# Keys of dilated attention stored by their residue modulo 16, in a hybrid decoder layer

## The chip, the cores and the metric

One NeuronCore of a Trainium2 chip runs the whole layer. The metric is device time in microseconds for one execution. Before the change the median of three runs is 2245.28 us (2243.73 to 2248.41).

## The reference

The layer takes x of 2048 tokens by 1024. After a norm, one projection feeds 8 attention heads and 8 heads of a gated linear recurrence (HGRN), each 64 wide; both outputs are normed, projected and added to x, and a two-level mixture of experts and a last norm follow. The change concerns the attention, which evaluates three dilated windows and mixes them by their log-sum-exp:

```python
DILATED_CONFIGS = ((128, 1), (512, 4), (2048, 16))
def dilated_branch(q, k, v, slopes, window, dilation):
    # query t attends keys t - j*dilation, j = 0..window/dilation
    ...
    scores = jnp.einsum('bgnqhd,bgnkhd->bgnhqk', qb, kk) / math.sqrt(Dh)
    bias = -slopes[:, None, None] * (sub_dist * dilation)[None]
    scores = jnp.where(valid, scores + bias, -jnp.inf)
    lse = jax.nn.logsumexp(scores, axis=-1)
    o = jnp.einsum('bgnhqk,bgnkhd->bgnqhd', jnp.exp(scores - lse[..., None]), vv)
```

For a branch of dilation d the tokens fall into d residue classes, and a block is 128 queries of one class against the 128 keys of its own block and the 128 before.

## The kernel before, in words

Heads are worked on in four pairs. For each pair the kernel projects v, q and k from a normed and transposed x (`v_tile`, `qk_chunk`), runs 48 attention blocks (`attention_steps`: 16 of branch 1, then 16 of branch 3, whose step is 16, then 16 of branch 2, whose step is 4; the names in the code are `br` 1, 3 and 2, with `DIL` their steps), and beside them projects and runs the pair's HGRN heads (`hgrn_steps`, `quad_steps`). Precision is held by splitting operands into a high and a low half of 16 bits.

`qk_chunk` projects 512 tokens into a PSUM tile ("proj", two buffers) and evacuates it for each of the two heads: ScalarE writes the high half (L358), VectorE the low half (L359). Tokens lie side by side in their own order, in `k` as in `qs`; for k, GpSimd's queue then copies both halves to the other 64 partitions (L361). `v_tile` leaves v in an SBUF tile V whose rows are tokens; branch 1 reads that tile itself. It is also spilled to DRAM (`vd`, L396), from where `load_v` reads it back in the row order of branch 3 and of branch 2 (L408, on SyncE's queue).

One block is `scores` and, three blocks later, `values`. `scores` issues four matmuls (L436): for each of the two heads the 128 queries are loaded as weights and the block's 128 or 256 keys stream through, once for the high and once for the low half of k. `block_cols` gives both operands as strided columns: a step of `dil` elements. The first block of a residue class has 128 keys, others 256; so branch 1 has one block of 128 and 15 of 256, branch 2 has 4 and 12, and branch 3 has 16 of 128. VectorE adds the bias and takes the maximum (L440), ScalarE exponentiates (L453, L455), VectorE forms the low half (L456), and a transposing DMA on SyncE's queue turns the result (PT, L458) for the value matmuls (L471, L473). `combine` joins the three branches, on VectorE and GpSimd, when a pair of blocks of branch 2 is done.

The bias is one table of distances d1, resident in SBUF, times a slope: `bias_tile` makes it for a branch (L422 on VectorE, L423 on GpSimd), at the pair's start for branch 1, and in the eighth block of branches 1 and 3 for the next branch.

TensorE's order is written out by a planner in the program (`Runner`), which takes each step with a fixed cost (a block's scores 430 ns, its values 330) and earliest times, and interleaves HGRN, projections and attention. The other engines' orders come from the tile scheduler by priority.

Of the kernel before, what the change touches and what calls it, by code (L numbers as in the profile page):

```python
# [16 lines left out]
OP = mybir.AluOpType  # L17
# [14 lines left out]
def shape_tables():  # L32

    p = np.arange(128)
    tt = p
    f = np.float32
    parts = {}
    parts['ident'] = np.eye(128, dtype=f)
    parts['ones'] = np.ones((128, 128), f)
    ch = tt >> 6  # L40
    same = ch[:, None] == ch[None, :]
    le = tt[:, None] <= tt[None, :]
    mid = ch * 64 + 31
    parts['cum'] = (same & le).astype(f) - (same & (tt[:, None] <= mid[None, :])).astype(f)
    parts['causal'] = (same & le).astype(f)
    sel = np.zeros((128, 4), f)
    for c in range(2):
        sel[:, 2 * c] = (ch == c) & (tt <= c * 64 + 31)
        sel[:, 2 * c + 1] = (ch == c) & (tt > c * 64 + 31)
    parts['sel'] = sel  # L50
    BIG = 2.0 ** 50
    def dist(tq, tk, dil):
        d = tq[:, None] - tk[None, :]
        ok = (d >= 0) & (d <= 128 * dil)
        return np.where(ok, d, BIG).astype(f)
    parts['d1'] = dist(128 + tt, np.concatenate([tt, 128 + tt]), 1)
# [12 lines left out]
    weight = np.stack([j < 2, j == 2, j < 3], 1).astype(f)  # L69
    parts['weight'] = np.repeat(weight, 32, 1)  # L70
    tok = 128 * np.arange(16)[None, :, None] + p[:, None, None] + 0 * np.arange(2)[None, None]
    parts['asg'] = np.stack([tok - tok % 16, tok % 16, 1 + 0 * tok], -1).reshape(128, 96).astype(f)
    parts['spare'] = np.stack([2048 + p, 2048 + 128 + p], 1).astype(f)
    off, cols = {}, 0
    for k, v in parts.items():
        off[k] = (cols, v.shape[1]); cols += v.shape[1]
    return np.ascontiguousarray(np.concatenate([parts[k] for k in parts], 1)), off
# [87 lines left out]
class Layer:  # L165
# [167 lines left out]
    def qk_chunk(self, D, W, which, ch, part):  # L333
        nc = self.nc
        XH, XL = self.XH[ch], self.XL[ch]
        wh, wl = W["qk"[which]]['wh'], W["qk"[which]]['wl']
        if ch == 0 and part == 0:
            if which == 0:
                D['q'] = [self.qk.tile([128, S], F16, name=f"qs{h}") for h in range(2)]
            else:  # L340
                D['k'] = [self.qk.tile([128, 2, S], F16, name=f"k{h}") for h in range(2)]
                self.scales(D, W)
        cs = slice(512 * ch, 512 * ch + 512)
        if part == 0:
            D['ps'] = self.psum([128, 512], "proj", 2)
        ps = D['ps']
        for k in range(2 * part, 2 * part + 2):
            nc.tensor.matmul(ps, wh[:, k, :], XH[:, k], start=(k == 0), stop=False)
            nc.tensor.matmul(ps, wh[:, k, :], XL[:, k], start=False, stop=False)
            nc.tensor.matmul(ps, wl[:, k, :], XH[:, k], start=False, stop=(k == KT - 1))  # L350
        if part < 3:
            return
        for h in range(2):
            a, b = slice(64 * h, 64 * h + 64), slice(64 - 64 * h, 128 - 64 * h)
            t = D["qk"[which]][h]
            hi, lo = (t[a, cs], t[b, cs]) if which == 0 else (t[a, 0, cs], t[a, 1, cs])
            sc = PSC / 2 if which == 0 and h == 0 else PSC
            nc.scalar.activation(hi, ps[a], AF.Copy, scale=sc)  # L358
            nc.vector.scalar_tensor_tensor(lo, ps[a], sc, hi, op0=OP.mult, op1=OP.subtract)  # L359
            if which == 1:  # L360
                nc.gpsimd.dma_start(t[b, :, cs], t[a, :, cs])  # L361

# [13 lines left out]
    def v_tile(self, D, W, n):  # L376
        nc = self.nc
        wh, wl = W['v']['wh'], W['v']['wl']
        if n == 0:
            D['V', 1] = self.vp.tile([128, NT, 2, 128], F16, name="V", bufs=2)  # L380
        if n % 4 == 0:
            D['vps'] = self.psum([128, 4, 128], "proj", 2)
        ps = D['vps'][:, n % 4]
# [5 lines left out]
        if n % 4 == 3:  # L389
            q = n // 4  # L390
            pv = D['vps'].rearrange("p n (h d) -> p n h d", h=2)
            vs = D['V', 1][:, 4 * q:4 * q + 4]
            nc.scalar.activation(vs[:, :, :, 0:64], pv, AF.Copy, scale=PSC)
            nc.vector.scalar_tensor_tensor(vs[:, :, :, 64:128], pv, PSC, vs[:, :, :, 0:64],  # L394
                                           op0=OP.mult, op1=OP.subtract)
            nc.gpsimd.dma_start(D['vd'][512 * q:512 * q + 512].rearrange("(n p) c -> p n c", p=128),  # L396
                                vs.rearrange("p n h c -> p n (h c)"))

    def load_v(self, D, br):

        nc, vd = self.nc, D['vd']
        V = D['V', br] = self.vp.tile([128, NT, 2, 128], F16, name="V", bufs=2)
        Vf = V.rearrange("p n h c -> p n (h c)")
        dil = DIL[br]
        for n in range(NT // dil):
            src = bass.AP(tensor=vd.tensor, offset=vd.offset + n * 128 * dil * 256,
                          ap=[[dil * 256, 128], [1, dil * 256]])
            nc.sync.dma_start(Vf[:, n * dil:n * dil + dil, :].rearrange("p n c -> p (n c)"), src)  # L408


    def block_cols(self, t, br, blk, keys):

        dil = DIL[br]
        r, n = blk % dil, blk // dil
        lo = n - 1 if keys and n else n
        return t[:, r + lo * 128 * dil:r + (n + 1) * 128 * dil - dil + 1:dil]

    def bias_tile(self, D, p, br):
        nc = self.nc
        b = D['bias', br] = self.ap_.tile([128, 256], F32, name="bias", bufs=2)  # L420
        col = self.asm.tile([128, 1], F32, name="slope")
        nc.vector.tensor_scalar(col, D['f'][:, 4:5], -DIL[br] * 2.0 ** -(2 * p + 2), None, op0=OP.mult)  # L422
        nc.gpsimd.tensor_scalar(b, self.c['d1'], col, 1.0, op0=OP.mult, op1=OP.mult)  # L423

    def scores(self, D, B, br, blk):
        nc = self.nc
# [4 lines left out]
        f, bias = D['f'], D['bias', br]  # L431
        ps = self.psum([128, 2, 256], "S", 2)
        for h in range(2):
            q = self.block_cols(D['q'][h], br, blk, False)
            for x in range(2):
                nc.tensor.matmul(ps[:, h, :W], q, self.block_cols(D['k'][h][:, x], br, blk, True), start=(x == 0),  # L436
                                 stop=(x == 1))
        mx = self.asm.tile([128, 2], F32, name="mx")
        for h in range(2):
# [383 lines left out]
    def attention_steps(self, p, D, st, A):  # L823
# [5 lines left out]
        def score(i):  # L829
            br, blk = seq[i]  # L830
            if i == 0:
                self.bias_tile(D, p, br)
            if blk == 8 and br != 2:
                self.bias_tile(D, p, {1: 3, 3: 2}[br])
            with self.tc.high_priority(offset=130):
                self.scores(D, B[i], br, blk)

# [384 lines left out]
    def route_setup(self, rb, ps):  # L1222
        nc, rp = self.nc, self.rpool
        _, off = shape_tables()
        self.load_consts(rp, off['before'][0], self.aps['cst'].shape[1], "ctr")
# [696 lines left out]
```

## Time and profile before

| what | value |
|---|---|
| median of 3 runs | 2245.28 us |
| the profiled execution | 2245.75 us |
| its span in the trace | 2243.9 us |
| mean granted TensorE clock | 0.946 |
| TensorE, VectorE, ScalarE, GpSimd busy | 89, 67, 54, 24% of the span |
| attention, first to last score matmul | 119.9 to 1117.1 us |

The abbreviations in the rows are PE for TensorE's matmuls, PEld for its weight loads (which overlap PE), DVE for VectorE, ACT for ScalarE, POOL for GpSimd, SP for SyncE; a q behind a name is an engine's queue of instructions that are not computation. L436 is line 436 of the kernel before. A row of a window gives its bounds and length, then the busy time (and the count of instructions) of PE, PEld, DVE, ACT and POOL, the granted TensorE clock as a share of 2.4 GHz, the mean busy share of the 16 DMA engines and GB/s. Matmuls are pipelined, so a matmul's duration is longer than its distance to the next one.

### The profile page before, as it was taken

To read this page: it belongs to the slowest core of one execution; us is meant where nothing else is said; L and a number is where in the kernel's file an instruction comes from. 1 tells how busy PE (TensorE), PEld (TensorE's weight loads), DVE (VectorE), ACT (ScalarE), POOL (GpSimd) and SP (SyncE) were. 2 spreads that over 40 slices of the span, in tenths; PEclk is the share of its full clock that TensorE was granted. 3 is DMA by queue.
4 is the path that set the end of the run, shared out by engine and by line. 5 is a ranking of instruction groups with operands and counts; after the bars stand their busy time and mean duration, and the time that the engine had idled before them with its cause. 6 is when DMAs were issued, how large, how long until landed. Compare 5 with 4: busy or idle time off the path is not lost. (4 is left out here: it accounts for less than half of the span.)

```text
span 2243.9 us, 39874 instructions
## 1 busy us (share of the span) xinstructions
PE 2000.7 (89%) x13777; PEld 1356.6 (60%) x13777; DVE 1500.7 (67%) x4211; ACT 1209.6 (54%) x2691; POOL 545.0 (24%) x620
## 2 busy tenths in 40 slices
PE   5998978999899998998888896999999999999981
PEld 4645565555755557554544444779999977766750
DVE  7657686778767696568876677665566656556525
ACT  6455653765547555666653433645555555555524
POOL 2312244033522235213331113021122321111110
PEclk9998988999999999999899996999999999999995
DMA  7234254533445235634579995899888999999857
GB/s 232 79 94 103 62 128 108 120 87 77 117 109 135 56 92 144 155 90 112 121 213 251 268 226 167 297 300 291 298 286 280 314 314 302 313 343 310 287 149 297
DMA packets 438896, 433.37 MB, mean 193 GB/s; under 512 B 242644, under 2 KB 325716, under 8 KB 438176
## 3 DMA queue, kind: packets, MB, share of 16 engines
q1 hardware_dynamic: 420464, 382.74, 55.8%
q0 software_dynamic: 14064, 46.46, 8.7%
q8 instruction: 108, 1.77, 0.3%
q10 hardware_dynamic: 4160, 1.58, 0.3%
q14 instruction: 100, 0.82, 0.1%
HBM read 305.30 MB, written 66.29 MB: 166 GB/s over the span
## 5 line engine op out<-in xcount | busy, mean ns | idle before, releaser
L1660 DVE TENSOR_TENSOR eL<-eraw,eH 128x1024 bf16<-128x1024 f32 x248 | 297.8, 1220 | 120.0 <-ACT eH L1654 114.5
L1654 ACT ACTIVATE eH<-eraw 128x1024 fp32r<-128x1024 f32 x252 | 258.5, 1053 | 110.5 <-PE acc L1746 59.0
L453 ACT ACTIVATE P<-S,orow,fqk 128x256 f32<-128x256 f32 (+1 forms) x384 | 195.2, 513 | 172.7 <-DVE orow L447 87.4
L567 PE MATMUL proj<-whh,x 128*128 128x512 f16 x512 | 202.6, 396 | 0.1
L568 PE MATMUL proj<-whl,x 128*128 128x512 f16 x512 | 201.2, 393 | 0.0
L569 PE MATMUL proj<-whh,x 128*128 128x512 f16 x512 | 199.9, 390 | 0.0
L1727 PE MATMUL acc<-xs,eH 128*128 128x352 f32 (+15 forms) x1216 | 196.0, 314 | 0.5 <-DVE xs L1705 0.5
L436 PE MATMUL S<-k,qs 128*128 128x256 f16 (+1 forms) x768 | 171.9, 355 | 14.1 <-ACT P L453 11.4
L1727 PEld LDWEIGHTS acc<-xs,eH 128*128 128x128 f32 x1216 | 176.1, 190 | 4.4 <-issue 2.4
L440 DVE CUSTOM_DVE_ANT_0 S<-S,bias 128x256 f32<-128x256 f32 (+1 forms) x384 | 141.3, 368 | 53.9 <-PE S L436 50.6
L456 DVE TENSOR_TENSOR Ps<-P,Ps 128x256 f16<-128x256 f32 (+1 forms) x192 | 130.6, 680 | 68.0 <-ACT Ps L455 65.1
L1829 POOL DMA_INDIRECT x2d<-yo,sidx x49 | 83.8, 1711 | 378.7 <-ACT xs L1704 98.1
L1777 PE MATMUL acc<-hs,eD 128*128 128x176 f32 (+15 forms) x1216 | 165.9, 296 | 1.1 <-DVE ts L1752 0.7
L1777 PEld LDWEIGHTS acc<-hs,eD 128*128 128x128 f32 x1216 | 160.5, 190 | 2.0 <-DVE ts L1752 1.0
L436 PEld LDWEIGHTS <-qs 128*128 128x128 f16 x768 | 89.2, 123 | 70.4 <-issue 22.8
L260 POOL TENSOR_TENSOR wraw<-wraw,g 128x1024 f32<-128x1024 f32 x44 | 84.8, 1929 | 167.2 <-DMA wraw<-in_w_in_dram 150.6
L1687 POOL DMA_INDIRECT xg<-h2d,gidx x49 | 54.7, 1117 | 268.8 <-PE tr L1701 249.0
L1745 PE MATMUL acc<-eH,xs 128*128 128x512 f32 x208 | 119.3, 574 | 0.0
L1789 PE MATMUL acc<-eD,hs 128*128 128x512 f32 x208 | 99.3, 616 | 20.5 <-ACT hs L1765 9.9
L386 PE MATMUL proj<-wh,x 128*128 128x128 f16 x512 | 95.0, 229 | 19.2 <-DVE V L394 19.2
L455 ACT ACTIVATE Ps<-P 128x256 f16<-128x256 f32 (+1 forms) x192 | 102.8, 535 | 6.0 <-DMA PT<-Ps 3.3
L658 POOL TENSOR_SCALAR sw<-Sp,hw 128x128 f32<-128x128 f32 x112 | 53.5, 478 | 197.0 <-DVE Sp L661 107.6
(396 smaller groups left out, 4960.4 us busy)
## 6 DMA issues: line engine op xcount, KB each, us to landing
eraw<-in_w_gate_dram SPq DMA_DIRECT2D x128, 512.0 KB
eD<-in_w_down_dram SPq DMA_DIRECT2D x128, 512.0 KB
eraw<-in_w_up_dram SPq DMA_DIRECT2D x124, 512.0 KB
wraw<-in_w_in_dram SPq DMA_DIRECT2D x41, 512.0 KB
od<-orow SPq DMA_DIRECT2D x64, 132.0 KB
R<-od SPq DMA_DIRECT2D x64, 132.0 KB
xt<-in_x_dram SPq DMA_DIRECT2D x16, 512.0 KB
wraw<-in_w_out_dram SPq DMA_DIRECT2D x16, 512.0 KB
```

What stands on the lines that cost most here:

```text
L436: nc.tensor.matmul(ps[:, h, :W], q, self.block_cols(D['k'][h][:, x], br, blk, True), start=(x == 0), stop=(x == 1))
L440: nc.vector.tensor_tensor_reduce(ps[:, h, :W], ps[:, h, :W], bias[:, 256 - W:256], 1.0, -3.0e38, OP.add, OP.max, mx[:, h:h + 1])
L453: nc.scalar.activation(P[:, h], ps[:, h, :W], AF.Exp, bias=nm[:, h:h + 1], scale=f[:, h:h + 1], accum_out=orow[:, 130 + h:131 + h])
L456: nc.vector.tensor_tensor(hv[:, 1], P, hv[:, 0], op=OP.subtract)
L567: nc.tensor.matmul(ps, self.XH[n // 4][:, k, ns], W['whh'][:, k, :], start=(k == 0), stop=False)
L568: nc.tensor.matmul(ps, self.XH[n // 4][:, k, ns], W['whl'][:, k, :], start=False, stop=False)
L569: nc.tensor.matmul(ps, self.XL[n // 4][:, k, ns], W['whh'][:, k, :], start=False, stop=(k == KT - 1))
L1654: nc.scalar.activation(H, raw, AF.Copy)
L1660: (nc.gpsimd if on_pool else nc.vector).tensor_sub(L, raw, H.bitcast(F32))
L1727: nc.tensor.matmul(gu[:, i, 0:2 * cap], w[:, o:o + 128], xs[:, k], start=(k == 0), stop=False, skip_group_check=True)
L1745: nc.tensor.matmul(gu[:, j], xs[:, k, 0], H[:, fs], start=(k == 0), stop=False)
L1777: nc.tensor.matmul(py[:, j, 0:cap], W['w_down', f][:, o:o + 128], hs[:, f], start=(f == 0), stop=(f == 3))
```

## The change

Inside each chunk of 512 tokens, k is now stored by residue modulo 16: token 16 a + r of the chunk stands at place 32 r + a. `qk_chunk` does it while evacuating, by reading the PSUM tile with a step of 16. Queries and their order stay. `block_keys` picks a block's keys from that order: for branch 3 one residue is a run of 32 in each of the four chunks; for branch 2 a class is four runs of 32 in each chunk; for branch 1, 128 tokens are 16 runs of 8. Since a block's keys then come in an order of their own, v's rows and the columns of the bias must follow. `load_v` reads v for branch 1 from DRAM too (16 loads a pair, four at each of blocks 0, 4, 8 and 12), and gives branch 2's rows another order. The distance table exists once for each branch, in DRAM, and is fetched by `bias_load` into the tile that `bias_tile` scales in place: at the pair's first block (pair 0 only), and in the eighth block of each branch for the next one.

```diff
+    for br, tk in ((1, 16 * (tt % 8) + tt // 8), (2, 4 * (tt % 32) + tt // 32), (3, tt)):
+        parts[f'd{br}'] = dist(128 + tt, np.concatenate([tk, 128 + tk]), 1)
...
+            src = ps[a]
+            if which == 1:
+                src = src.rearrange("p (a r) -> p r a", r=16)
+                hi, lo = (x.rearrange("p (r a) -> p r a", r=16) for x in (hi, lo))
             sc = PSC / 2 if which == 0 and h == 0 else PSC
-            nc.scalar.activation(hi, ps[a], AF.Copy, scale=sc)
-            nc.vector.scalar_tensor_tensor(lo, ps[a], sc, hi, op0=OP.mult, op1=OP.subtract)
+            nc.scalar.activation(hi, src, AF.Copy, scale=sc)
+            nc.vector.scalar_tensor_tensor(lo, src, sc, hi, op0=OP.mult, op1=OP.subtract)
...
-    def load_v(self, D, br):
+    def load_v(self, D, br, g=0):
...
+        if br == 1:
+            for n in range(4 * g, 4 * g + 4):
+                src = bass.AP(tensor=vd.tensor, offset=vd.offset + n * 128 * 256,
+                              ap=[[256, 16], [16 * 256, 8], [1, 256]])
+                nc.sync.dma_start(Vf[:, n], src)
+            return
+        rows = [[4 * 256, 4], [16 * 256, 32]] if br == 2 else [[dil * 256, 128]]
         for n in range(NT // dil):
-            src = bass.AP(tensor=vd.tensor, offset=vd.offset + n * 128 * dil * 256,
-                          ap=[[dil * 256, 128], [1, dil * 256]])
+            src = bass.AP(tensor=vd.tensor, offset=vd.offset + n * 128 * dil * 256, ap=rows + [[1, dil * 256]])
...
+    def block_keys(self, t, br, blk):
+
+        r, n = blk % DIL[br], blk // DIL[br]
+        t = t.rearrange("p (g r a) -> p g r a", g=4, r=16)
+        if br == 3:
+            return t[:, :, r]
+        if br == 2:
+            return t.rearrange("p g (q c) a -> p c g q a", c=4)[:, r, max(n - 1, 0):n + 1]
+        cols = [t[:, m // 4, :, 8 * (m % 4):8 * (m % 4) + 8] for m in (n - 1, n) if m >= 0]
+        if len(cols) == 1:
+            return cols[0]
+        a, b = cols
+        return bass.AP(tensor=a.tensor, offset=a.offset, ap=[a.ap[0], [b.offset - a.offset, 2], *a.ap[1:]])
+
+    def bias_load(self, br):
+        a = shape_tables()[1][f'd{br}'][0]
+        self.dist = self.ap_.tile([128, 256], F32, name="bias", bufs=2)
+        self.nc.sync.dma_start(self.dist, self.aps['cst'][:, a:a + 256])
...
-        b = D['bias', br] = self.ap_.tile([128, 256], F32, name="bias", bufs=2)
+        b = D['bias', br] = self.dist
...
-        nc.gpsimd.tensor_scalar(b, self.c['d1'], col, 1.0, op0=OP.mult, op1=OP.mult)
+        nc.gpsimd.tensor_scalar(b, b, col, 1.0, op0=OP.mult, op1=OP.mult)
...
-                nc.tensor.matmul(ps[:, h, :W], q, self.block_cols(D['k'][h][:, x], br, blk, True), start=(x == 0),
+                nc.tensor.matmul(ps[:, h, :W], q, self.block_keys(D['k'][h][:, x], br, blk), start=(x == 0),
...
             if i == 0:
+                if p == 0:
+                    self.bias_load(1)
                 self.bias_tile(D, p, br)
-            if blk == 8 and br != 2:
-                self.bias_tile(D, p, {1: 3, 3: 2}[br])
+            if br == 1 and blk % 4 == 0:
+                self.load_v(D, 1, blk // 4)
+            if blk == 8 and (br != 2 or p < self.last_pair):
+                self.bias_load({1: 3, 3: 2, 2: 1}[br])
+                if br != 2:
+                    self.bias_tile(D, p, {1: 3, 3: 2}[br])
```

How instructions move: TensorE issues the same instructions in the same order as before; only the lines' numbers change. On SyncE's queue, this is the end of pair 0 and the start of pair 1 before (R and mix belong to `combine`, V is v's tile and vd_65 its spill, wraw the weights being loaded, PT the turned probabilities):

```order
L506 DMA R<-od_68 128x264
L259 DMA wraw<-in_w_in_dram 128x8x128
L458 DMA_TRANSPOSE PT<-Ps 128x8x128
L259 DMA wraw<-in_w_in_dram 128x8x128
L534 DMA mix<-orow 128x2x128
L408 DMA V<-vd_65 128x4096
L534 DMA mix<-orow 128x2x128
L710 DMA mix<-qT 128x4x128
L458 DMA_TRANSPOSE PT<-Ps 128x4x128
```

and in the changed kernel:

```order
L538 DMA R<-od_68 128x264
L448 DMA bias<-in_cst_dram 128x256
L261 DMA wraw<-in_w_in_dram 128x8x128 x2
L490 DMA_TRANSPOSE PT<-Ps 128x8x128
L566 DMA mix<-orow 128x2x128
L417 DMA V<-vd_65 128x1x256 x4
L422 DMA V<-vd_65 128x4096
L566 DMA mix<-orow 128x2x128
L742 DMA mix<-qT 128x4x128
L417 DMA V<-vd_65 128x1x256 x12
L490 DMA_TRANSPOSE PT<-Ps 128x4x128
```

Branch 1's sixteen loads of v stand between the last combined blocks of pair 0 and the first transposed probabilities of pair 1, four of them ahead of branch 3's load and of the last store of a combined block; the bias for pair 1's first branch comes earlier still.

On GpSimd, the making of branch 3's bias in pair 0 stood like this before (sw is the product by which HGRN's state is carried from one step to the next, Sp that state):

```order
L260 TENSOR_TENSOR wraw<-wraw,g_100 128x1024
L658 TENSOR_SCALAR sw<-Sp,hw 128x128
L423 TENSOR_SCALAR bias<-cta,slope 128x256
L658 TENSOR_SCALAR sw<-Sp,hw 128x128 x6
L260 TENSOR_TENSOR wraw<-wraw,g_100 128x1024
```

and in the changed kernel:

```order
L262 TENSOR_TENSOR wraw<-wraw,g_100 128x1024
L690 TENSOR_SCALAR sw<-Sp,hw 128x128 x2
L455 TENSOR_SCALAR bias<-bias,slope 128x256
L690 TENSOR_SCALAR sw<-Sp,hw 128x128 x5
L262 TENSOR_TENSOR wraw<-wraw,g_100 128x1024
```

It stays among the seven products of one quad of HGRN, one product later, and now reads the tile that the DMA fills.

## Rows read from the trace of the kernel before

**Rows 1.** The page, part 1: busy us (share of the span) and instructions.
```profile
PE 2000.7 (89%) x13777; PEld 1356.6 (60%) x13777; DVE 1500.7 (67%) x4211; ACT 1209.6 (54%) x2691; POOL 545.0 (24%) x620
```

**Rows 2.** Windows, pair 1, branches 1, 3, 2: engines' busy, clock, DMA share, GB/s.
```profile
382.00:437.00 55.00, 52.81 (x358) 29.25 (x357) 39.81 (x127) 36.54 (x97) 3.61 (x6) 1.00 0.45 104
437.00:500.00 63.00, 60.40 (x368) 35.32 (x366) 44.79 (x165) 41.73 (x121) 15.41 (x17) 1.00 0.40 93
500.00:587.00 87.00, 79.11 (x510) 46.62 (x508) 73.54 (x280) 50.68 (x147) 33.58 (x49) 0.92 0.35 83
```

**Rows 3.** Waits of PE, 120:1120: us in total, times, longest.
```profile
PE proj L386 <- DVE V L394: 19.2, 3, 11.4
PE hg L672 <- ACT dS L647: 16.6, 13, 3.0
...
PE hg L697 <- DVE Am L684: 10.3, 4, 5.1
...
PE S L436 <- DMA k<-k: 2.4, 2, 1.7
```

**Rows 4.** Timeline, PE, branch 1 of pair 1: start us, duration us.
```profile
382.24 0.39 PE L436 MATMUL S<-k,qs 128*128 128x128 f16 x4
382.47 0.38 PE L348 MATMUL proj<-x,wh 128*128 128x512 f16 x1
...
411.46 0.60 PE L436 MATMUL S<-k,qs 128*128 128x256 f16 x4
411.89 0.38 PE L348 MATMUL proj<-x,wh 128*128 128x512 f16 x1
```

**Rows 5.** Timeline, PE, branch 3 of pair 1.
```profile
442.18 1.10 PE L436 MATMUL S<-k,qs 128*128 128x128 f16 x4 [0.18 <-ACT P L453]
443.10 0.40 PE L567 MATMUL proj<-whh,x 128*128 128x512 f16 x1
```

**Rows 6.** Timeline, PE, branch 2 of pair 1.
```profile
519.88 0.64 PE L436 MATMUL S<-k,qs 128*128 128x128 f16 x4
520.34 0.24 PE L471 MATMUL O<-V,PT 128*128 128x128 f16 x1
...
549.16 1.07 PE L436 MATMUL S<-k,qs 128*128 128x256 f16 x4
550.05 0.40 PE L567 MATMUL proj<-whh,x 128*128 128x512 f16 x1
```

**Rows 7.** Groups by form, L436's weight loads, branches 1, 3, 2.
```profile
L436 PEld LDWEIGHTS <-qs 128*128 128x128 f16 x64 | 5.9, 97 | 6.4 <-issue 3.5
...
L436 PEld LDWEIGHTS <-qs 128*128 128x128 f16 x64 | 9.1, 149 | 5.2 <-issue 0.6
...
L436 PEld LDWEIGHTS <-qs 128*128 128x128 f16 x64 | 7.2, 120 | 6.6 <-issue 2.2
```

**Rows 8.** By line, k's evacuation, POOL's bias: ns min/median/max; bias's waits.
```profile
L358 ACT ACTIVATE k<-proj x32: 573/592/593, 68.0 to 948.8; 64x512 f16<-64x512 f32 x32
...
L359 DVE SCALAR_TENSOR_TENSOR k<-proj,k x32: 675/688/695, 68.6 to 950.3; 64x512 f16<-64x512 f32 x32
...
L423 POOL TENSOR_SCALAR bias<-cta,slope x12: 472/482/908, 72.3 to 969.7; 128x256 f32<-128x256 f32 x12
...
  DVE mx L440: 25.6, 6
```

**Rows 9.** Window of the qkv projections of pair 2, columns as in rows 2.
```profile
587.00:645.00 58.00, 51.10 (x560) 39.34 (x559) 34.66 (x80) 24.20 (x44) 32.53 (x31) 0.97 0.47 135
```

**Rows 10.** By line, SP's issues of v's loads: ns min/median/max.
```profile
L408 SPq DMA_DIRECT2D V<-vd x20: 327/432/573, 115.3 to 984.0; - x20
```

**Rows 11.** DMA, 120:1120: queue's packets, MB, share; issues, KB, us to landing.
```profile
q1 hardware_dynamic: 236720, 97.55, 40.3%
...
k<-k POOLq DMA_DIRECT2D x26, 128.0 KB, 2.5
vd<-V POOLq DMA_DIRECT2D x12, 256.0 KB, 2.9
```

More of the change, by code (lines that the diff above doesn't have):

```diff
@@ L55, in dist @@
         return np.where(ok, d, BIG).astype(f)
-    parts['d1'] = dist(128 + tt, np.concatenate([tt, 128 + tt]), 1)
     bc = lambda a: np.broadcast_to(np.asarray(a, f), (128, len(a))).copy()
@@ L379, in v_tile @@
         if n == 0:
-            D['V', 1] = self.vp.tile([128, NT, 2, 128], F16, name="V", bufs=2)
+            D['V'] = self.vp.tile([128, NT, 2, 128], F16, name="V", bufs=2)
         if n % 4 == 0:
@@ L391, in v_tile @@
             pv = D['vps'].rearrange("p n (h d) -> p n h d", h=2)
-            vs = D['V', 1][:, 4 * q:4 * q + 4]
+            vs = D['V'][:, 4 * q:4 * q + 4]
             nc.scalar.activation(vs[:, :, :, 0:64], pv, AF.Copy, scale=PSC)
@@ L397, in v_tile @@
                                 vs.rearrange("p n h c -> p n (h c)"))
-    def load_v(self, D, br):
+    def load_v(self, D, br, g=0):
         nc, vd = self.nc, D['vd']
-        V = D['V', br] = self.vp.tile([128, NT, 2, 128], F16, name="V", bufs=2)
+        if g == 0:
+            D['V', br] = self.vp.tile([128, NT, 2, 128], F16, name="V", bufs=2)
+        V = D['V', br]
         Vf = V.rearrange("p n h c -> p n (h c)")
         dil = DIL[br]
+        if br == 1:
[5 more added lines that the diff above has]
+        rows = [[4 * 256, 4], [16 * 256, 32]] if br == 2 else [[dil * 256, 128]]
@@ L405, in load_v, with block_queries @@
         for n in range(NT // dil):
-            src = bass.AP(tensor=vd.tensor, offset=vd.offset + n * 128 * dil * 256,
-                          ap=[[dil * 256, 128], [1, dil * 256]])
+            src = bass.AP(tensor=vd.tensor, offset=vd.offset + n * 128 * dil * 256, ap=rows + [[1, dil * 256]])
             nc.sync.dma_start(Vf[:, n * dil:n * dil + dil, :].rearrange("p n c -> p (n c)"), src)
-    def block_cols(self, t, br, blk, keys):
+    def block_queries(self, t, br, blk):
         dil = DIL[br]
@@ L414, in block_cols @@
         r, n = blk % dil, blk // dil
-        lo = n - 1 if keys and n else n
-        return t[:, r + lo * 128 * dil:r + (n + 1) * 128 * dil - dil + 1:dil]
+        return t[:, r + n * 128 * dil:r + (n + 1) * 128 * dil - dil + 1:dil]
+    def block_keys(self, t, br, blk):
[10 more added lines that the diff above has]
+        return bass.AP(tensor=a.tensor, offset=a.offset, ap=[a.ap[0], [b.offset - a.offset, 2], *a.ap[1:]])
@@ L433, in scores @@
         for h in range(2):
-            q = self.block_cols(D['q'][h], br, blk, False)
+            q = self.block_queries(D['q'][h], br, blk)
             for x in range(2):
-                nc.tensor.matmul(ps[:, h, :W], q, self.block_cols(D['k'][h][:, x], br, blk, True), start=(x == 0),
+                nc.tensor.matmul(ps[:, h, :W], q, self.block_keys(D['k'][h][:, x], br, blk), start=(x == 0),
                                  stop=(x == 1))
@@ L1224, in route_setup @@
         _, off = shape_tables()
-        self.load_consts(rp, off['before'][0], self.aps['cst'].shape[1], "ctr")
+        self.load_consts(rp, off['before'][0], off['d1'][0], "ctr")
         self.gf = rp.tile([128, DM], F32, name="gf")
```

## The prediction

> **What bounds the kernel now.** I read the page's busy shares first: TensorE (PE) is busy for 2000.7 of 2243.9 us, VectorE (DVE) for 1500.7 [rows 1]. That is an average over unlike stages, so I went to the stage that the change touches, the attention of a head pair, and asked for the windows of pair 1's three branches [rows 2]. Branch 1 (step 1) takes 55 us with PE busy 52.81, branch 3 (step 16) 63 us with PE busy 60.40, branch 2 (step 4) 87 us with PE busy 79.11: the first two are bound by PE (96% busy), while in branch 2 DVE stands at 73.54 of 87, 85%, and PE idles 7.9 us. Pairs 2 and 3 repeat this. The table of waits over the whole attention part (120 to 1120 us) shows what PE waits for when it does: mostly evacuations by DVE and ScalarE (ACT); for the keys only 2.4 us in all [rows 3].
>
> Next, what a score matmul costs. The ends of matmuls are modelled, so I take the distance between starts in the timeline: from the first of a block's four score matmuls to the next foreign matmul. In branch 1, 256 contiguous keys: 411.46 to 411.89, 0.43 us; 128 keys: 382.24 to 382.47, 0.23 us [rows 4]. In branch 3, 128 keys at steps of 16: 442.18 to 443.10, 0.92 us, four times the price of the same 128 columns [rows 5]. In branch 2, 256 keys at steps of 4: 549.16 to 550.05, 0.89 us, and 128 keys: 519.88 to 520.34, 0.46 us, twice the price [rows 6]. In branch 2 the price goes with the width, so it is the keys' streaming that is slow. At 256 columns in a matmul, 0.89 us is 0.87 ns a column against 0.42 contiguous; branch 3 has 1.80 ns. One reading fits all three: keys come in units of 16 bytes, and a fresh unit costs about 1.8 ns, whether one of its elements is used (branch 3) or two (branch 2); eight of them, 8 x 0.42 = 3.4 ns, hide it.
>
> The weight loads tell a second thing. The queries stay strided, and their loads take a mean of 97 ns in branch 1, 149 in branch 3 and 120 in branch 2 [rows 7].
>
> **The change, part by part.** *Branch 3's keys* become runs of 32 contiguous elements. The matmul itself could then start 56 ns after the one before (0.23 us for four, [rows 4]). But the load of the strided queries remains: one of 97 ns allows a distance of 56, so I let the excess of 52 ns count in full, 108 ns. Three of the four distances hold such a load, the fourth a contiguous one: 3 x 108 + 56 = 0.38 us for a block, 0.54 saved, and 64 blocks (16 in each of 4 pairs) make 34.6 us. The bounds: the load is hidden entirely, 0.23, 44 us; or its 149 ns are all serial, 3 x 149 + 56 = 0.50, 27 us.
>
> *Branch 2's keys* become runs of 32 too. 48 blocks of 256 go from 0.89 to 0.43: 22.1 us; a load of 120 ns, worth a distance of 79, fits beneath a matmul of 108. The 16 blocks of 128 go from 0.46 to 3 x 79 + 56 = 0.29 (79 being 56 plus the excess of 23), 2.7 us, with bounds of 0 and, at 0.23, 3.7.
>
> *Branch 1's keys* become runs of 8, 16 bytes each, 64 bytes apart. No row shows this form. The least it can cost is what it costs now, 0.43; the most I take from the step of 4, 0.89, which would lose 60 x 0.46 = 27.6 us. I take nothing, because in the reading above eight elements take longer than one fresh line.
>
> Here a rule speaks against the change. The trace prices a step of 4 at twice the contiguous one [rows 4, 6]. The Trainium skill, SBUF — State Buffer, section Door 1: The DMA port swizzle, says that SBUF is read in lines of 16 bytes, that two hits in a line suffice for full bandwidth, and that a step of 8 bf16 is therefore free. By that rule branch 2's term would be 0 and the sum of the three branches 34.6. By the row it is 59.4, and the row decides.
>
> So PE gets **59.4 us** less to do (bounds 49 and 70, branch 1 aside). PE's order of instructions is the same, so what is left is how much turns into waiting. After the change branch 3 takes 63 - 8.7 = 54 us in a pair; DVE's 44.79 us there become 83% of it. Branch 1 at 72% DVE (39.81 of 55) leaves PE idle 4%, branch 2 at 85% leaves it 9% [rows 2]; at 83% I expect some 8%, 4.5 us in place of 2.6, so 2 lost in a pair, **8** in all. Branch 2 saves 6.2 us in a pair; all of it would put DVE at 73.54 of 81, 91%. Its PE waits already are for ACT's dS and DVE's Am and V [rows 3], whose work does not shrink: I let half be lost, **12** in all.
>
> *Evacuating k*: 32 ACT and 32 DVE operations now read PSUM at steps of 16 floats. They take 592 and 688 ns for 512 columns [rows 8], 1.16 and 1.34 ns a column. No row has such a read. Bounds: no change, or four times as long as for PE's keys at that step. A fresh line at 1.8 ns would make them about 0.9 us, 0.3 more for each on engines that are 42% and 60% busy in the stretch of the projections (587 to 645 us, [rows 9]). I take nothing on the path.
>
> *v through DRAM for branch 1*: 16 more loads for a pair on SP's queue, at 432 ns of issue each [rows 10], 6.9 us. They stand ahead of the pair's first transposes of P and wait for the last read of branch 2's v; the store of the last combined block is right behind some of them. The spill that they read back lands 2.9 us after issue [rows 11], and the qkv projections of the next pair lie in between. The 64 loads of 64 KB are 4.2 MB beside the 97.55 MB that the same queue moves in this part, in 40.3% of the 16 engines' time [rows 11]. Hidden; if the cover went, 6.9 us in each of 4 pairs. Branch 2's v rows move in another order at the same size, a whole branch ahead of their use.
>
> *The distance tables* come by DMA, 12 of 128 KB; GpSimd's (POOL) scaling is unchanged in work (482 ns) but now waits for a landing of about 2.5 us (the 128 KB copy of k, [rows 11]) in the 8 that are issued just before. It already waited 25.6 us over 6 of them for DVE [rows 8], and SP issues earlier than that. Behind it on POOL stand the products sw of HGRN's states, for which DVE waits. Bounds 0 and 8 x 2.5 = 20 us; I take **2**.
>
> Sum: 59.4 - 8 - 12 - 2 = 37 us. The profiled execution took 2245.75 us, its span 2243.9; that is 0.5 over the median of the three runs, 2245.28. 2245.75 - 37 = 2208.75, against the median 2208.
>
> **The rivals.**
> *All of it arrives* (0.14): waits don't grow, since branch 1 shows PE at 96% with heavier DVE operations per block. 59.4, with the load's best case up to 70: 2176 to 2186.
> *DVE takes the bound* (0.13): branch 2 gives nothing, branch 3 half, 17 - 2 = 15 us, 2230. For it: the 85%; against it: DVE idles 13.5 of 87 us there.
> *Runs of 8 cost in branch 1* (0.07): a jump costs 1.8 ns on top of eight columns; 32 jumps in 256 columns are 58 ns, and 4 matmuls in each of 60 blocks make 4 x 60 x 58 ns = 14 us: 2222. At the outer bound 2236.
> *The scores do not speed up in branch 3* (0.04), because the strided query load sets the distance of 0.23 us, not the keys: then only branch 2's 12 - 2 remain, 2235. Against it: a load of 149 ns leaves some 80 of the 230 ns between two starts.
> *A step of 4 is free and branch 2 gains nothing* (0.03): its 0.89 would have another cause; 34.6 - 8 - 2 = 25 us, 2221. This is what the page's rule would do here; rows 6 speak against it.
> *Slower* (0.06): the strided PSUM read of k's evacuation. At four times the price a chunk's chain of one ACT and two DVE operations goes from 0.59 + 2 x 0.69 = 2.0 to 7.9 us, 16 chunks in all. DVE is 60% busy there; if half of the 5.9 us reaches PE, which holds two PSUM buffers, 16 x 2.9 = 47 us are lost: 2255. From 37 / 16 = 2.3 us a chunk on it decides. Against it: nothing else in the trace reads that way, but both engines already spend longer on a column than PE does.
>
> **How the numbers follow.** My forecast, 2208, has 0.53, its own range 2195 to 2222. The range for 8 in 10 leaves out the slower case, the far end of the full gain, the worst of the DVE and branch 1 cases and the 2235 of unchanged branch 3 scores: 2182 to 2233. About 0.2%, 4.5 us, is what a measurement of this kernel can tell from no change. Faster by more than that: all but the slower case and a tail of the DVE, branch 1 and branch 3 cases, 0.87. Within it 0.06. Slower 0.07: the 0.06 and 0.01 for mishaps together.
>
> **What would show it.** Right: branch 3's four scores at about 0.38 us and branch 2's at 0.43, branch 1's still 0.43; query loads still near 149 and 120 ns; the three windows shorter by about 7, 3 and 0 us in a pair; PE's waits for dS, Am and V up by some 20 us. Wrong: branch 1 above 0.5; branch 3 at 0.9; k's evacuation well over 1 us with PE waiting for it; the first transposes of a pair late behind loads of v; POOL stalled at a bias.

## The result, and the profile after

The changed kernel takes **2263.27 us** (median of 4 runs, 2260.56 to 2265.94) against 2246.85 us for the kernel before in the same comparison: ratio 1.0068, 95% interval 1.0049 to 1.0086. By this ratio it is 15 us slower (the medians are 16.4 apart), where 37 us less were forecast. The profiled execution took 2260.56 us, its span 2258.7.

The first thing to read is that the change did to TensorE what it set out to do. The page's busy shares, against [rows 1]:

```profile
PE 1953.8 (86%) x13753; PEld 1338.8 (59%) x13777; DVE 1493.7 (66%) x4211; ACT 1206.6 (53%) x2691; POOL 547.6 (24%) x620
```

TensorE's busy time fell by 46.9 us, and the span grew by 14.8. The scores themselves, in the timeline of TensorE for pair 1 (start us, duration us; a block's four score matmuls, then the next instruction), branch 1, branch 3, branch 2:

```profile
411.09 0.60 PE L468 MATMUL S<-k,qs 128*128 128x256 f16 x4
411.52 0.38 PE L350 MATMUL proj<-x,wh 128*128 128x512 f16 x1
...
441.50 0.41 PE L468 MATMUL S<-k,qs 128*128 128x128 f16 x4 [0.61 <-ACT P L485]
441.74 0.38 PE L599 MATMUL proj<-whh,x 128*128 128x512 f16 x1
...
521.75 0.39 PE L468 MATMUL S<-k,qs 128*128 128x128 f16 x4
521.97 0.22 PE L503 MATMUL O<-V,PT 128*128 128x128 f16 x1
...
550.29 0.60 PE L468 MATMUL S<-k,qs 128*128 128x256 f16 x4
550.73 0.38 PE L599 MATMUL proj<-whh,x 128*128 128x512 f16 x1
```

Branch 1 costs 0.43 us a block as before [rows 4]; branch 3 went from 0.92 [rows 5] to 0.24; branch 2 from 0.89 and 0.46 [rows 6] to 0.44 and 0.22. Over 64, 48 and 16 blocks these are 43.5 + 21.6 + 3.8 = 69 us of matmul distance saved at full clock, close to the upper bound of the prediction (70). The query loads are as slow as they were [rows 7] (group by form, weight loads of the scores in branch 3 of pair 1), and k's stepped evacuation costs nothing [rows 8] (by line, ns min/median/max):

```profile
L468 PEld LDWEIGHTS <-qs 128*128 128x128 f16 x65 | 6.5, 149 | 4.6 <-issue 2.8
```
```profile
L364 ACT ACTIVATE k<-proj x32: 573/592/592, 68.9 to 971.9; 64x512 f16<-64x512 f32 x32
...
L365 DVE SCALAR_TENSOR_TENSOR k<-proj,k x32: 675/688/695, 69.5 to 973.0; 64x512 f16<-64x512 f32 x32
```

So where did 69 us go? One window over the whole attention part, from its first score matmul to the last block's, answers that (bounds and length in us, PE's busy time and count, granted clock, DMA share, GB/s). Before:

```profile
119.90:1116.40 996.50, 904.70 (x6387) 0.94 0.44 105
```

and after:

```profile
122.30:1137.00 1014.70, 859.35 (x6387) 0.92 0.48 108
```

The part is 18.2 us longer. PE's busy time is 45.4 us less, not 69, because the granted clock was 0.92 in place of 0.94 (a mean over stretches at 2.4 and at 1.2 GHz: by the trace's record of the clock, 163.8 us of the part are at 1.2 GHz after and 119.5 before, and half of the difference is 22 us). And PE's time without work went from 996.5 - 904.70 = 91.8 to 155.4 us: 63.6 more. What it waited for, in the table of PE's waits from 110 to 1150 us (us in total, times, longest; compare [rows 3]; dS, hq, sg, qT and Am are tiles of the HGRN part, V is v's, P holds the exponentials):

```profile
PE O L503 <- DMA PT<-Ps: 27.3, 17, 5.4
PE proj L392 <- DVE V L400: 19.4, 3, 10.0
PE hg L704 <- ACT dS L679: 18.9, 13, 2.1
PE S L468 <- ACT P L485: 18.0, 19, 2.8
```

The longest sum is new: values waiting for turned probabilities, 27.3 us, where the same window of the kernel before has 3.8:

```profile
PE O L471 <- DMA PT<-Ps: 3.8, 4, 1.3
```

In branch 3 of pair 1 one such wait is followed by half clock (timeline of PE; projections 0.21 us apart before it, 0.42 after it):

```profile
457.70 0.38 PE L600 MATMUL proj<-whl,x 128*128 128x512 f16 x1
457.91 0.38 PE L601 MATMUL proj<-whh,x 128*128 128x512 f16 x1
463.66 0.29 PE L503 MATMUL O<-V,PT 128*128 128x128 f16 x1 [5.37 <-DMA PT<-Ps]
...
463.97 0.61 PE L599 MATMUL proj<-whh,x 128*128 128x512 f16 x1
464.38 0.63 PE L600 MATMUL proj<-whl,x 128*128 128x512 f16 x1
```

That is the point at which branch 2's v is being loaded. The DMA view of 453 to 467 us (busy tenths of the 16 DMA engines in 40 slices of 0.35 us), before:

```profile
DMA  1096999848998998610000000158799999999000
```

and after, with GB/s below:

```profile
DMA  0122593999222222222222222332568899999992
GB/s 35 47 88 99 193 296 122 309 159 100 105 99 105 99 105 94 88 76 88 99 99 105 94 97 79 79 105 64 145 164 224 236 316 266 210 211 194 161 93 83
```

Before, the load of 1 MB fills the engines (8 and 9 tenths) and its 512 packets of 2048 bytes are moved between 453.7 and 459.3 us. After, the share is 2 tenths, four engines' worth of sixteen (the trace has four of these packets in flight at once for most of the time), at some 100 GB/s for 5 us on end, and the same packets take from 452.9 to 466.2 us: 13.3 us in place of 5.6. The new pattern leads with a dimension of 4 (four residues, then 32 rows each). The Trainium skill, DMA: Bandwidth & Descriptors, section Why a DMA increments its semaphore by 16 and not by 1, says that a transfer is spread over the largest number of engines up to 16 that divides the slowest dimension of both sides; the trace agrees with the 4 which that gives here.

### The profile page after: what moved, and what is told of

Its sections match the earlier page's. It is cut to its first block, busy times and chain, and to the rows that moved or that the text cites. A ratio compares the mean times of both kernels' runs of the same rounds, so it can differ in the third digit from the quotient of the medians.

```text
span 2258.7 us, 39943 instructions
## 1 busy us (share of the span) xinstructions
PE 1953.8 (86%) x13753; PEld 1338.8 (59%) x13777; DVE 1493.7 (66%) x4211; ACT 1206.6 (53%) x2691; POOL 547.6 (24%) x620
## 5 line engine op out<-in xcount | busy, mean ns | idle before, releaser
L599 PE MATMUL proj<-whh,x 128*128 128x512 f16 x512 | 205.7, 402 | 2.0 <-ACT hq L606 2.0
L601 PE MATMUL proj<-whh,x 128*128 128x512 f16 x512 | 204.0, 398 | 0.0
L262 POOL TENSOR_TENSOR wraw<-wraw,g 128x1024 f32<-128x1024 f32 x44 | 84.4, 1919 | 176.7 <-DMA wraw<-in_w_in_dram 163.8
L468 PE MATMUL S<-k,qs 128*128 128x256 f16 (+1 forms) x768 | 105.7, 262 | 24.3 <-ACT P L485 18.0
L468 PEld LDWEIGHTS <-qs 128*128 128x128 f16 x768 | 77.4, 123 | 63.6 <-issue 34.6
L503 PE MATMUL O<-V,PT 128*128 128x128 f16 x600 | 80.7, 226 | 27.4 <-DMA PT<-Ps 27.3
```

What stands on the lines that cost most here:

```text
L468: nc.tensor.matmul(ps[:, h, :W], q, self.block_keys(D['k'][h][:, x], br, blk), start=(x == 0), stop=(x == 1))
L599: nc.tensor.matmul(ps, self.XH[n // 4][:, k, ns], W['whh'][:, k, :], start=(k == 0), stop=False)
L601: nc.tensor.matmul(ps, self.XL[n // 4][:, k, ns], W['whh'][:, k, :], start=False, stop=(k == KT - 1))
```

## The experiments

All ratios are to runs of the kernel before on the same chip, and us gained or lost are worked out from the ratio; the difference of two medians can be 4 us off it. The names of lines differ from kernel to kernel; the tiles' names don't. The theory that they test: the keys' order gains something, less than the matmuls promise, and the two sets of loads that it entails cost more than that.

**The keys alone.** The kernel before with the new order of k, and v and the table as they were, so that in branches 1 and 2 they meet the keys in another order.

```diff
 (against the changed kernel)
-        if br == 1:
...
-        rows = [[4 * 256, 4], [16 * 256, 32]] if br == 2 else [[dil * 256, 128]]
+                          ap=[[dil * 256, 128], [1, dil * 256]])
...
-    def bias_load(self, br):
...
+        nc.gpsimd.tensor_scalar(b, self.c['d1'], col, 1.0, op0=OP.mult, op1=OP.mult)
```

> The kernel before, with k alone stored and read by residue; v's rows and the distance table stay in token order, so the attention's output is another function. No new load, no bias by DMA. Theory A (branch 2's four loads of v, whose row pattern leads with 4, run long and hold up the transposes of P): the scores' gain is real, 2205 to 2228 us, and TensorE's wait for the transposed P stays at a few us. Theory B (TensorE's freed time turns into waits for VectorE and ScalarE and the waits lower its clock): 2250 to 2264 us, as the changed kernel. Theory C (the loads of v for branch 1 or the biases by DMA hold up SyncE or GpSimd): as A.

Measured: 2236.17 us (10 runs), ratio 0.9955, 0.994 to 0.997: 10 to 11 us gained of the 69, which lies between the ranges of theories A and B. Its window (the profile is of the fastest of the ten executions, 2229.22 us) over the attention part, and PE's waits from 110 to 1150 us:

```profile
119.30:1105.00 985.70, 856.44 (x6388) 0.92 0.44 106
```
```profile
PE S L454 <- ACT P L471: 20.6, 22, 2.8
...
PE hg L690 <- ACT dS L665: 19.3, 13, 3.2
PE hg L633 <- ACT hq L619: 13.3, 4, 3.7
...
PE hg L661 <- DVE sg L640: 7.4, 6, 2.0
...
PE O L489 <- DMA PT<-Ps: 6.7, 10, 1.8
```

985.7 us, 10.8 less than before. PE is busy 48.3 us less (again at 0.92, where 0.02 of 985.7 are 20 us) and without work for 129.3 us, 37.5 more: 69 - 20 - 37.5 is 11.5. The waits have no single owner. ACT's P is waited for 20.6 us (11.4 before), dS 19.3 (16.6), hq 13.3 (8.9), sg 7.4 (none listed before), and PT only 6.7 (3.8).

Cut into stages, the four pairs together show where the gain goes. Branch 3, counted from its first score to the first of branch 2, is 21.2 us shorter, half of the 43.5 that its matmuls save. Branch 2, up to its last block, is 5.9 us longer, although its matmuls save 25, and the three stretches between pairs are 4.7 us longer. Pair 1 as an example (branch 3, branch 2, then the stretch to pair 2; length, PE busy, granted clock), before and with the keys alone:

```profile
438.00:502.10 64.10, 61.49 (x376) 1.00 0.39 92
502.10:580.70 78.60, 70.71 (x434) 0.91 0.34 81
580.70:645.10 64.40, 57.50 (x626) 0.97 0.46 131
```
```profile
429.80:489.50 59.70, 51.17 (x375) 1.00 0.42 97
489.50:570.30 80.80, 68.88 (x435) 0.87 0.32 78
570.30:639.20 68.90, 61.10 (x625) 0.90 0.48 125
```

The lower clock is not this one profile's: the mean granted clock of the ten executions is 0.936 to 0.942, that of the 20 of the kernel before beside them 0.942 to 0.949.

**The loads alone.** Everything of the change but the keys' order; k stays in token order beneath v and tables in the new one.

```diff
 (against the changed kernel)
-            src = ps[a]
-            if which == 1:
-                src = src.rearrange("p (a r) -> p r a", r=16)
...
-                nc.tensor.matmul(ps[:, h, :W], q, self.block_keys(D['k'][h][:, x], br, blk), start=(x == 0),
+                nc.tensor.matmul(ps[:, h, :W], q, self.block_cols(D['k'][h][:, x], br, blk, True), start=(x == 0),
```

> The changed kernel with k stored and read as before (token order, strided columns), but with all its new loads: v for branch 1 from DRAM, v's rows for branch 2 in the new order, the distance tables by DMA; since v and tables keep the new order, the output is another function. Theory A: slower than before by 25 to 60 us, 2270 to 2305, with waits for the transposed P of some 5 us at the start of each branch 3. Theory B: 2245 to 2254. Theory C: slower too, but with the waits elsewhere (k's copy, the bias, the start of branch 1).

Measured: 2270.12 us (4 runs), 1.0116, 1.0083 to 1.0149: 26 us lost, a time in theory A's range. Keys alone and loads alone add up to 1.0071; the change shows 1.0068. PE's waits for turned probabilities are 10.7 us here, 2.4 the longest, so the 5 us at each branch 3 that theory A names are not there; the 27.3 us of the changed kernel come only with the faster keys.

**Branch 2's v order alone.** The kernel before with one edit, by which branch 2's probabilities meet v's rows in another order.

```diff
-                          ap=[[dil * 256, 128], [1, dil * 256]])
+        rows = [[4 * 256, 4], [16 * 256, 32]] if br == 2 else [[dil * 256, 128]]
...
+            src = bass.AP(tensor=vd.tensor, offset=vd.offset + n * 128 * dil * 256, ap=rows + [[1, dil * 256]])
```

> The kernel before with one edit: branch 2's v is read back in the new row order (pattern led by 4, then 32); its values are mixed up by that, the work is the same. Theory A: the whole cost of e2, 2265 to 2300 us. Theory B: 2245 to 2250. Theory C: 2245 to 2252.

Measured: 2261.62 us (5 runs), 1.0073, 1.005 to 1.0095: some 16 us for a permutation of rows at the same size, less than theory A's range and more than B's and C's. The DMA view of 453 to 467 us has the same picture as after, and PE's waits from 110 to 1150 us have more for turned probabilities (3.8 before):

```profile
DMA  9000000690012222864992222922222222223322
```
```profile
PE O L471 <- DMA PT<-Ps: 10.1, 8, 2.6
```

The time is lost where that load runs: branch 3 is 2.8, 5.8 and 4.7 us longer in pairs 0 to 2. In pair 1 PE waits for turned probabilities for 5.8 us of it (1.3 before), and its clock is 0.98 there in place of 1.00; pair 0 shows no such wait (there hq is waited for 1.8 us longer).

**The same rows by other loads.** The changed kernel, branch 2's v read by 16 loads with 32 rows each, a few at a time in branch 3. What is computed is that of the change.

```diff
-        rows = [[4 * 256, 4], [16 * 256, 32]] if br == 2 else [[dil * 256, 128]]
+        if br == 2:
+            for q in range(4):
+                src = bass.AP(tensor=vd.tensor, offset=vd.offset + g * 512 * 256 + q * 4 * 256,
+                              ap=[[16 * 256, 32], [1, 1024]])
+                nc.sync.dma_start(Vf[32 * q:32 * q + 32, 4 * g:4 * g + 4, :].rearrange("p n c -> p (n c)"), src)
+            return
...
-                self.load_v(D, 2)
+                self.load_v(D, 2, 0)
+            if br == 3 and blk in (2, 5, 8):
+                self.load_v(D, 2, 1 + (blk - 2) // 3)
```

> The changed kernel with branch 2's v read by four loads of 32 rows for each chunk in place of one of 4 x 32, and chunks 1 to 3 issued at blocks 2, 5 and 8 of branch 3. Theory A: 2208 to 2232 us, the waits for the transposed P gone from branch 3. Theory B: 2255 to 2264, as the change. Theory C: 2250 to 2263.

Measured: 2256.29 us (10 runs), 1.0037, 1.0022 to 1.0052. About half of the 0.68% is back, less than theory A's range asks. The edit changes two things at once, the loads' shape and the blocks at which they are issued. PE's waits from 110 to 1150 us show the PT wait gone (27.3 to 6.7) and others still grown:

```profile
PE hg L731 <- DVE Am L722: 18.4, 6, 7.1
...
PE hg L721 <- ACT qT L712: 13.3, 3, 6.0
PE O L509 <- DMA PT<-Ps: 6.7, 9, 1.9
```

**The distance tables earlier.** On top of that, `bias_load` at block 2 in place of 8.

```diff
-            if blk == 8 and (br != 2 or p < self.last_pair):
+            if blk == 2 and (br != 2 or p < self.last_pair):
```

> The kernel of e4 (branch 2's v in four loads of 32 rows) with the distance tables fetched at block 2 of a branch in place of block 8; GpSimd scales them where it did. Theory C (GpSimd's waits for the table, 35.9 us over 4 of them in e2, hold up HGRN's states): 2244 to 2252 us, against e4's 2256. Rival, the waits are hidden by GpSimd's slack: within 3 us of e4.

Measured: 2256.61 us (6 runs), 1.0044, 1.0027 to 1.0061. No difference, but the edit does not test the theory, for it left the tables' loads where they were. The program keeps two tiles for the bias, and in the trace a load goes out about where one branch ends and the next begins, when a tile comes free, and before block 2 of the next (in pair 0 at 182.4 us, where branch 3 begins at 186.0; in the kernel of the run before at 181.3 and 185.2), not in the eighth block as the program has it written. GpSimd's waits for the tables are the same without and with the edit (table of its waits from 110 to 1150 us):

```profile
POOL bias L461 <- DMA bias<-in_cst_dram: 35.8, 4, 21.5
```
```profile
POOL bias L461 <- DMA bias<-in_cst_dram: 35.5, 4, 21.4
```

What these waits cost is open.

**Branch 1's loads alone.** The kernel before, with v for branch 1 from DRAM.

```diff
+            if br == 1 and blk % 4 == 0:
+                self.load_v(D, 1, blk // 4)
```

> The kernel before, with one part of the change: v for branch 1 is spilled and read back by 16 loads of 64 KB a pair (in the change's row order; keys, tables and branch 2's rows as before, so branch 1's probabilities meet v's rows in another order). Theory A: these 16 issues (432 ns each, 6.9 us) stand on SP ahead of the loads of raw weights, which come late, and with them the last projections of the next pair; that is the rest between all the loads (ratio 1.0116) and branch 2's rows alone (1.0073), some 10 us: 1.002 to 1.006, 2252 to 2261 us, with the stretch between two pairs longer by 2 to 5 us and PE's wait for qT grown there. Theory B (the prediction's word 'hidden'): 0.999 to 1.001, no stretch changed, and the rest belongs to the distance tables' loads and to POOL.

Measured: 2256.43 us (12 runs), 1.0036, 1.0019 to 1.0052: some 8 us lost, as theory A has it. One place is the stretch between two pairs. SP's timeline of the kernel before, from the last score of pair 1 (580.7 us) on, has raw weights for HGRN as soon as their buffer is free, 34.6 us into the stretch:

```profile
615.31 14.51 SPq L259 DMA_DIRECT2D wraw<-in_w_in_dram  x4
```

With branch 1's loads (its stretch begins at 577.6 us):

```profile
610.02 5.48 SPq L411 DMA_DIRECT2D V<-vd  x8
615.60 1.16 SPq L259 DMA_DIRECT2D wraw<-in_w_in_dram  x2
```

Eight loads of v hold the queue until 615.5 us, 38 us into the stretch. GpSimd then waits for the weights 3.08 us in place of 1.08 before the one at 619.91, the products sw of HGRN stand behind that, and PE, which waited 3.0 us for qT in this stretch before, waits 5.0 (GpSimd's timeline, and the table of PE's waits from 577.6 to 648.6 us):

```profile
619.91 1.90 POOL L260 TENSOR_TENSOR wraw<-wraw,g 128x1024 f32<-128x1024 f32 x1 [3.08 <-DMA wraw<-in_w_in_dram]
```
```profile
PE hg L691 <- ACT qT L682: 5.0, 1, 5.0
```

The stretch takes 71.0 us where it took 64.4: PE is without work for 3.3 us more of it, and the rest goes with a clock of 0.93 in place of 0.97. The other stretches fit. From pair 0 to pair 1 no raw weights stand behind the loads of v, and the stretch keeps its 40.8 us; from pair 2 to pair 3 two stand behind eight of them, and it takes 72.1 us in place of 69.2. That the weights' delay is all of the 8 us is not shown, for this stretch is longer also where no load was added (68.9 us, with a clock of 0.90, with the keys alone).

One sum stays open. Keys alone and these loads alone would give 0.9991; the changed kernel with branch 2's v in 16 loads has 1.0037, some 10 us more than that and clear of the intervals. What it adds to the two are those 16 loads, the tables and their joint effect with faster keys; neither the 16 loads nor the tables ran alone.

**What the freed time in branch 2 is worth.** The kernel with the keys alone, branch 2's four score matmuls issued twice (the second pass writes the same sums again).

```diff
-            for x in range(2):
+            for x in (0, 1, 0, 1) if br == 2 else (0, 1):
```

> The kernel of e1 (keys alone by residue) with branch 2's four score matmuls issued twice (the second time from the start again), so that TensorE is as long at them as before the change, 0.87 us for a block of 256 keys. Theory B (in branch 2 TensorE's freed time only becomes waiting, and the waiting lowers the clock): no slower than e1, 2225 to 2240 us. Theory D (the freed time is worth what it measures): 22 us more than e1, 2254 to 2262.

Measured: 2246.6 us (12 runs), 0.9988, 0.9973 to 1.0004. Another 48 x 0.44 + 16 x 0.22 = 25 us of matmuls cost 0.33%, 7 us: neither nothing nor all, and between the two ranges. Here branch 2's matmuls take about as long as before the change and branch 3's as long as after it; by the interval, the 43.5 us saved in branch 3 are worth 0.27%, 6 us, at most.

**No loads: PE writes the scores in token order.** v and the table stay in token order if the scores do. The keys come in the new order and the matmul's output goes to PSUM at steps.

```diff
-                nc.tensor.matmul(ps[:, h, :W], q, self.block_keys(D['k'][h][:, x], br, blk), start=(x == 0),
+                nc.tensor.matmul(self.score_cols(ps[:, h, :W], br, nk), q, self.block_keys(D['k'][h][:, x], br, blk), start=(x == 0),
```

> The kernel of e1 with the matmuls writing branch 1's and 2's scores to PSUM in token order (a step of 16 or 4 floats between columns), so that v and the distances need no new order and no new load. If stepped writes cost TensorE nothing: 2228 to 2242 us, e1's time. If they cost what stepped reads of keys cost (branch 1 to 0.89 us a block or more): 2262 to 2290.

Measured: 2237.79 us (6 runs), 0.9955, 0.9938 to 0.9972: faster than both kernels, and in the range for writes that cost nothing. But they do cost. A stepped write costs nearly as much as a stepped read of the keys (0.89): a block of branch 1 takes 0.82 us in place of 0.43 (timeline of PE), and yet the attention part (the window below it) is only 4.3 us longer than with the keys alone, PE being busy for 29.6 us more of it.

```profile
377.43 1.03 PE L461 MATMUL S<-k,qs 128*128 128x256 f16 x4
378.25 0.42 PE L348 MATMUL proj<-x,wh 128*128 128x512 f16 x1
```
```profile
119.40:1109.40 990.00, 886.07 (x6388) 0.94 0.45 106
```

**No loads: DVE and ACT read the scores in token order.** The same with contiguous writes and stepped reads. For it the keys of a block's two halves are taken in turn, residue by residue.

```diff
+            s = self.by_token(ps[:, h, :W], br, True)
+            nc.vector.tensor_tensor_reduce(s, s, self.by_token(bias[:, 256 - W:256], br, False), 1.0, -3.0e38, OP.add,
...
+            nc.scalar.activation(self.by_token(P[:, h], br, False), self.by_token(ps[:, h, :W], br, True), AF.Exp, bias=nm[:, h:h + 1], scale=f[:, h:h + 1],
```

> The kernel of e1 with the scores left in the stored order in PSUM, and VectorE's bias and maximum and ScalarE's exponential reading them there by token (steps of 16 to 64 floats); what they write of P is in token order, so v and the distances need no new order and no new load. If those reads are free, as k's evacuation was (592 and 688 ns, unchanged): 2228 to 2242 us, e1's time. If they take half as long again: 2250 to 2275.

Measured: 2241.07 us (10 runs), 0.9963, 0.9943 to 0.9983, in the range for reads that cost nothing. The stepped reads are free: in branch 1 of pair 1 the groups by form have 427 and 559 ns, the same to the nanosecond as before.

```profile
L465 DVE CUSTOM_DVE_ANT_0 S<-S,bias 128x256 f32<-128x256 f32 x29 | 12.4, 427 | 0.4
...
L478 ACT ACTIVATE P<-S,orow,fqk 128x256 f32<-128x256 f32 x28 | 15.6, 559 | 15.9 <-DVE orow L472 11.8 <-issue 1.3 <-DVE Ps L481 1.0
```
```profile
L440 DVE CUSTOM_DVE_ANT_0 S<-S,bias 128x256 f32<-128x256 f32 x29 | 12.4, 427 | 0.4
...
L453 ACT ACTIVATE P<-S,orow,fqk 128x256 f32<-128x256 f32 x28 | 15.6, 559 | 15.5 <-DVE orow L447 6.9 <-issue 5.9 <-DVE Ps L456 1.0
```

**Both: branch 1 read, branch 2 written.** `by_token` for branch 1, `score_cols` for branch 2.

> The keys stored as in the change, no load added: in branch 1 VectorE and ScalarE read the scores in token order (as in e10), in branch 2 PE writes them in token order (as in e9, 216 ns a matmul). PE has 26 us less to do than in e9 and 20 more than in e1 and e10. Theory A (time that PE gains or loses in branches 1 and 2 mostly turns into waiting and a lower clock, and back): no clear difference from e1, e9 and e10, 0.994 to 0.997, 2234 to 2241 us. Theory B (e9's stepped writes in branch 1 cost their 26 us, and what bounds these kernels is PE): 10 us or more below e9, 0.988 to 0.992, 2215 to 2228 us. Branch 1's stretches 56 to 57 us (e9: 59.4).

Measured: 2241.78 us (12 runs), 0.9964, 0.995 to 0.9977, as theory A has it. No gain on either, though PE is busy for 20 us less of the attention part than where it writes both (886.07, above):

```profile
120.90:1108.50 987.60, 866.14 (x6387) 0.94 0.45 106
```

PE's time without work is 121.5 us here, 103.9 where it writes both, 129.3 with the keys alone: what PE saves, it waits.

## Why the prediction was wrong

It missed in the sign, and the result lies outside its range. Its account was 59.4 us saved on PE, 20 lost to waits, 2 to the bias, nothing to the loads. The runs give 69 saved, some 58 lost to waits and clock (11 left, by the run with the keys alone), and 26 lost to the loads. Of the 52 us between forecast and result the loads make 26 and the waits and the clock 38; the keys' larger saving and the 2 us set down for the bias take 12 back. So two steps failed: with the loads at nothing, as forecast, the change would have gained 11 us and not 37.

- **The keys' streaming**: right. Runs of 32 and of 8 stream at the contiguous price in all three branches. The term was mis-sized in branch 3, where the 52 ns by which a stepped query load is longer were counted in full: 0.24 us a block, not 0.38. The loads still take 149 ns and hide beneath the other matmuls.
- **"A step of 4 is free and branch 2 gains nothing"** fell: its blocks went from 0.89 to 0.44 us, so what the prediction cites from the Trainium skill, SBUF — State Buffer, section Door 1: The DMA port swizzle, does not hold for keys that stream into a matmul; **"Runs of 8 cost in branch 1"** and **"The scores do not speed up in branch 3"** fell too.
- **"Slower", by k's evacuation**: fell. 592 and 688 ns, unchanged. That the change is slower all the same is by another mechanism, and no credit to this rival.
- **"Branch 2's v rows move in another order at the same size, a whole branch ahead of their use"**: this is the step that turned the gain into a loss. Size and lead time were right and beside the point. The load's shape set how many DMA engines carry it, and while four of them were full for 13.3 us the transposes of P, which the values of branch 3 need at once, came late. This edit alone costs 0.73%; that it is the shape and not the order of rows as such rests on the DMA views and on the run with other loads, which changed their timing too.
- **"Hidden"**, of branch 1's loads: failed as well. The prediction had the 6.9 us of issue, and behind them on SP the transposes of P and the combined block's store; the raw weights, which GpSimd and then HGRN wait for in the stretches from pair 1 on, were not among them. The order that it had looked at, from pair 0 to pair 1, has none behind these loads. Alone they cost 0.36%.
- **The distance tables** (2 us): not told from nothing; what the loads alone lose beyond the two single runs is 0.0116 - 0.0073 - 0.0036 = 0.0007, within intervals that would hide 10 us as well. No run shows their price.
- **"8" and "12" lost to waits**: far too little, 37.5 in the run with the keys alone, and this is the larger of the two failures. Half of branch 2's gain was let go; all of it went, for branch 2 became longer. The waits were taken from DVE's busy share, and their owners from a table of the whole part: in branch 2 of pair 1 PE waited for hq (3.1 us) and dS (2.5), not for V, which stands in the stretches between pairs. The waits named, dS, Am and V, grew by some 4 us together and not by 20; P, hq and sg grew by 27. This points to chains through several engines (scores, maximum, exponential; HGRN's hq, sg, dS) whose length does not shrink when PE is faster; no run shortened such a chain. And one loss was in no term: PE, idle more often, is granted 2.4 GHz for less of the time, 0.92 against 0.94, some 20 us.

That the lower clock follows from the idling is argued from the timeline (half clock sets in behind a wait) and from the run in which PE writes stepped scores: it is without work for 25 us less than with the keys alone, and its clock is 0.94 again (0.944 to 0.949 over its six whole executions). But the clock is 0.94 also where branch 1 is read, with 121.5 us without work, so the sum of idle time is not all that sets it. No run changed the clock by itself. What part of the 58 us a different planner's order could win back wasn't tried.

## What to carry to other kernels

A permutation of rows in a DMA is not free because the bytes are the same: look at the leading dimension of the new pattern, and at whatever else needs those engines in the time that it then takes, here 13 us in place of 6. Where data must meet in one order, first ask which access permutes for nothing; here it was the read of PSUM by VectorE and ScalarE, which needs no load at all. And in a part where PE is 91% busy but three engines pass work around, price a saving on PE at what the nearest chain leaves of it: here about one us in six.

## What the runs showed of the hardware

- A matmul that writes PSUM at steps of 4 or of 16 floats takes 216 ns from start to start in place of 109 for 256 columns: twice, whichever step. The Trainium skill, PSUM — Partial Sum Buffer, section Specifications (TRN2), says that an access that is not contiguous slows matmuls; the trace agrees, and adds that VectorE's and ScalarE's stepped reads of the same tile cost nothing (427 and 559 ns, either way).
- Weight loads of 149 ns, stepped by 16, leave 0.24 us for a block's four score matmuls, some 60 ns each: they overlap almost wholly.
- Keys at a step cost the same at either clock: in the kernel before, three blocks of branch 3 inside stretches of 1.2 GHz (from 183.9, 202.7 and 204.0 us on) take 0.93 to 0.96 us, against 0.92 at 2.4 GHz. Keys in runs do not: 0.41 to 0.43 us for such a block with the keys alone at 1.2 GHz, 0.24 at 2.4. So the change saves less wherever the clock is low.
